# An unnormalised first column pair of w_in between two halves of the PLE rows, h in two lagged steps, and T1 of w_out split ahead of B22

## The chip, the core and the metric

The kernel runs on one core of one Trainium2 chip. Times are device microseconds (us) of one execution of the whole program, from the hardware profiler. TensorE does the matmuls (PE in the profile), VectorE is DVE, ScalarE is ACT, GpSimd is POOL, SyncE (SP) issues most of the DMAs. The kernel before was timed three times; the figure that counts is the median of such runs, beside the same for the changed kernel.

## The reference, cut to what matters

One layer of a decoder trunk on 1024 tokens of 1024 channels, in float32:

```python
h = rms_norm(x, g_pre)                               # x * g_pre * rsqrt(mean(x*x) + eps), per token
s5_x, s5_g, lru_x, lru_g, gate_s, gate_l = split(h @ w_in)
y_s = s5_ssm(s5_x, ...)                              # needs s5_x = the first 512 columns of w_in
z_s = (glu(gelu(y_s) @ w_glu) * silu(s5_g)) @ w_bs
z_l = (rg_lru(conv(lru_x)) * silu(lru_g)) @ w_bl
merged = sigmoid(gate_s) * z_s + sigmoid(gate_l) * z_l
x = x + rms_norm(merged @ w_out, g_post)
x = x + (p @ w_ple) * sigmoid(x @ w_ple_gate)
```

Two things in it matter here. The factor rsqrt(mean(x*x)) is one number per token, and a product h @ w is linear in it, so it may be applied to the product instead of to h. And p @ w_ple (called the PLE rows below) depends on nothing else, so it may be done at any time.

## The kernel before, in words

**Layout.** Channels lie on the 128 partitions, tokens on the free axis. x is eight tiles `xt(k)` of 128 x 1024. A column of a weight matrix is 128 output channels; its weights come in blocks of 128 x 128, and four blocks are a quad. A product over all 1024 channels is a sum over k = 0 to 7.

**Three matmuls for one.** Every float32 factor a is split into a high part of fp32r type (`hi`, a copy by ACT) and the rest (`lo` = a - hi, a subtraction, on DVE as a rule). `three` (L306) then issues three matmuls of 128 x 128 by 128 x 512: high by high (L308), high weight by low data (L309), low weight by high data (L310).

**Weights.** The class `Weights` loads raw blocks through SP into four buffers, makes the high part on ACT (L215, `make`) and the low part on DVE (L227, `lows`), in a ring of six quads `wq`. `QUADS` is the order of the quads over the whole kernel and so the order of all the weight work; `ahead` and, early on, `weights(upto)` make quads ahead of their use. For w_out a variant of Strassen's method is used: POOL forms sums of weight blocks (`wS`, L187), and the data side has the operands B11, B21, T2, T3, T1, B22 and T4, which are quarters of `merged` or their sums and differences. `op_split` (L1156) splits such an operand, the high part on ACT (L1150) or by a DVE copy (L1148), the low part on DVE (L1157).

**Order of the work.** There is no scheduler here: PE, DVE, ACT and POOL each execute in the order in which the program is written, and an instruction that waits holds all that stand behind it on its engine. Background generators in the list `bg` (S5, operand splits) are advanced one step by each `tick()`, which the matmul loops call after each group of matmuls.

The stages around the change are, in order:
- the eight PLE rows (L693 to L712), 12 matmuls each on a quad of w_ple, evacuated by ACT (L710) from one of three PSUM row buffers `pw2` to SBUF and stored in DRAM. Beside them ACT squares x (L683), DVE adds the squares up into `ssq` (`sdp`, L685) and steps through the parameter work of S5, `s5_params`, a generator of some 54 steps (`prep`), which is small DVE work until a sine table on ACT (L596, L597) and a chain on POOL (L604 to L661) that DVE waits for once (L632);
- the token statistics, `tok_rstd` (L375): PE sums the squares over the channels (L380), DVE and ACT make the reciprocal root, PE spreads it over the partitions into two PSUM banks `psb_pre` (L400);
- h: `h_hi` (L726) computes x * g_pre * rstd on DVE (L729, with the factor in PSUM) and its high part on ACT (L730), `h_build` (L732) the low parts, on DVE for the first 512 tokens and on POOL for the second (L739);
- u0, columns 0 and 1 of w_in (`two`, L343, 96 matmuls), with `h_build` called ahead of each k, then u2, columns 2 and 3, likewise. `u_out` (L745) copies a column of the result with a strided ACT instruction (L748) and stores it for S5;
- many further columns of w_in, S5, the LRU heads and the projections, which the change leaves alone but for the time at which S5 starts: its generator `s5_all` runs in the ticks behind u2;
- w_out: four products X with B11, two with B21, then per row pair the products Y (T2), Z (T3), W (T1) and V (B22), each 12 matmuls (`product`, L1263). The operands T1 and B22 are made by the generator `out_ops` (L1217), four steps in `bg` that are queued behind the four B11 products.

Of the kernel before, what the change touches and what calls it, by code (L numbers as in the profile page):

```python
# [9 lines left out]
F32 = mybir.dt.float32  # L10
# [7 lines left out]
P = 128  # L18
# [18 lines left out]
def weight_plan():  # L37
# [208 lines left out]
def tile_hybrid_trunk(  # L246
# [218 lines left out]
    sqs = [two_rows(i, f"sqs{i}") for i in (0, 1)]  # L465
    ple_sb = [two_rows(i, f"ple_sb{i}") for i in (4, 5, 13, 2)]
# [50 lines left out]
    W.fetch(7)  # L517
# [146 lines left out]
    seen = []  # L664

    def prep_steps(n):
        for _ in range(n):
            next(prep, None)

    def prep_exp(n):  # L670
        for _ in range(n):
            if not seen:
                seen.extend(["exp"] * (next(prep) == "exp"))

    def prep_until(mark):
        while next(prep, mark) != mark:
            pass

    prep_exp(24)

    def square(k):
        sq = sqs[k % 2][:, k // 2 % 2] if k else ssq
        S.activation(sq, xt(k), AF.Square)  # L683
        if 0 < k < ND - 1:
            V.tensor_tensor(ssq, ssq, sq, ALU.add)  # L685
            prep_exp(5)
        return sq

# [3 lines left out]
    squares = {0: (0,), 1: (1, 2), 2: (3,), 3: (4,), 4: (5, 6), 5: (7,)}  # L692
    for m in range(ND):  # L693
        if m % 2 == 0:
            wb = W.next()
        if m == 7:
            prep_exp(100)
            next(stats)
# [4 lines left out]
        for k in squares.get(m, ()):  # L703
            sq = square(k)
            if k == ND - 1:
                ssqs.append(sq)
        if m == 7:
            next(stats)
        sb = ple_sb[m // 2][:, m % 2]
        S.activation(sb, ps, AF.Copy)  # L710
        nc.sync.dma_start(ple_d[m], sb)
        if m in (1, 3, 5, 6):  # L712
            weights({1: 2, 3: 3, 5: 5, 6: 7}[m])
        if m == 3:
            W.fetch(11)
    for _ in stats:
        pass

    hq = {n: [quarter(page(i0 + j, f"h{n}{j}")) for j in range(2)]
          for n, i0 in (("B11", 0), ("B21", 4), ("B12", 10), ("B22", 12))}  # L720

    def hplain(k, h):
        hi, lo = hq[f"B{1 + k // 4}{1 + h}"]
        return hi[:, k % 4, :], lo[:, k % 4, :]

    def h_hi(k):  # L726
        for h in range(2):
            xs = xt(k, HALF[h])
            V.scalar_tensor_tensor(xs, xs, gpre[:, k:k + 1], rb[h], ALU.mult, ALU.mult)  # L729
            S.activation(hplain(k, h)[0], xs, AF.Copy)  # L730

    def h_build(k):  # L732
        if k == 0:
            h_hi(0)
        elif 0 < k < ND - 1:
            h_hi(k + 1)
# [3 lines left out]
        if k <= 0:  # L740
            h_hi(k + 1)
        if k == ND - 1:
            prep_until("den")

    def u_out(m, ps, tile):  # L745
        for h in range(2):
            up = tile(h).rearrange("p (j k) -> p j k", j=8)
            S.activation(up.rearrange("p j k -> p k j"), ps[h].rearrange("p (k j) -> p k j", j=8), AF.Copy)  # L748
# [3 lines left out]
    ups = quarter(page(9, "ups", F32))  # L752
# [691 lines left out]
```

## Time and profile before

| | us |
|---|---|
| three runs | 981.36, 982.51, 982.83 |
| median | 982.51 |
| the profiled execution, its time | 978.07 |
| the profiled execution, its span | 976.3 |
| PE busy in the span | 948.3 |
| DVE busy | 586.0 |
| ACT busy | 455.7 |
| POOL busy | 160.5 |

How to read it: the span runs from the first instruction to the last of one profiled execution; its time holds 1.8 us more around that. PE is busy for all but 28.0 us of the span, so what a change to the order of the work can move lies in a few places: the time before PE's first matmul, the waits of PE between two matmuls, and stretches in which the clock granted to TensorE is lower. In a timeline row the first number is the start and the second the duration; a row that ends with "xN" joins N instructions of one kind. Matmuls overlap, so their rate is read from start to start.

### The profile page before, as it was taken

How to read it: one execution, taken by the hardware profiler on the slowest of the kernel's cores; microseconds unless marked ns; L12 is line 12 of the kernel's file. 1: busy time of each engine (PE TensorE's matmuls, PEld its weight loads, DVE VectorE, ACT ScalarE, POOL GpSimd, SP SyncE). 2: the span in 40 equal slices, each digit the busy share in tenths (PEclk: the TensorE clock that was granted, in tenths of full speed). 3: DMA queues.
4: the chain of work that ended last, by engine and by line, in shares of the span. 5: the costliest groups of instructions: out<-in, count | busy, mean ns of one | idle time of the engine just before them, and what ended most of it. 6: DMA issues, size and time to landing. Idle time of an engine off the chain costs nothing.

```text
span 976.3 us, 11808 instructions
## 1 busy us (share of the span) xinstructions
PE 948.3 (97%) x4304; PEld 776.9 (80%) x4304; DVE 586.0 (60%) x1017; ACT 455.7 (47%) x654; POOL 160.5 (16%) x177
## 2 busy tenths in 40 slices
PE   7899999999999999999999999999999998999988
PEld 5788777888788888888888888888888876887766
DVE  7853777888761236666666668345311577786832
ACT  7542244334432146666766665233112344458461
POOL 0255421211100000000000000000001345433431
PEclk9999999999999999999999999999999999999999
DMA  9634232333242211111111115742348995399995
GB/s 349 244 80 127 93 101 85 114 115 114 72 118 99 81 49 49 49 49 49 48 49 49 49 40 153 260 151 70 108 135 233 246 194 178 106 244 228 282 267 125
DMA packets 64282, 128.19 MB, mean 131 GB/s; under 512 B 18400, under 2 KB 29024, under 8 KB 64224
## 3 DMA queue, kind: packets, MB, share of 16 engines
q1 hardware_dynamic: 55584, 109.61, 34.4%
q0 software_dynamic: 8640, 17.83, 10.4%
q8 instruction: 34, 0.56, 0.2%
q14 instruction: 24, 0.20, 0.1%
HBM read 84.81 MB, written 27.79 MB: 115 GB/s over the span
## 4 chain that ended last, share of the span: by engine, by line
PE 74%; DVE 11%; issue 6%; DMA 4%; POOL 2%; ACT 1%; SPq 0%; POOLq 0%; DVEq 0%; ACTq 0%
PE ps_L L308 4%; PE ps_L L310 4%; PE ps_L L309 4%; PE ps_rx L308 4%; PE ps_rg L308 4%; PE ps_rg L310 4%; PE ps_rx L310 4%; PE ps_rx L309 4%; PE ps_rg L309 4%; PE ps_bl L310 4%; PE ps_bl L309 4%; PE ps_bl L308 4%; PE ps_pg L310 2%; DMA wq<-wraw 2%; PE ps_pg L309 2%
## 5 line engine op out<-in xcount | busy, mean ns | idle before, releaser
L215 ACT ACTIVATE wq<-wraw 128x512 fp32r<-128x512 f32 (+1 forms) x189 | 112.3, 607 | 96.5 <-PE ps_bl L310 77.3
L219 POOL DMA_DIRECT2D wq<-wraw x52 | 47.9, 920 | 550.6 <-ACT wq L218 527.3
L308 PE MATMUL ps_L<-hB,wq 128*128 128x512 f32 x320 | 127.2, 398 | 0.0
L310 PE MATMUL ps_L<-hB,wq 128*128 128x512 f32 x320 | 124.8, 390 | 0.0
L309 PE MATMUL ps_L<-hB,wq 128*128 128x512 f32 x320 | 124.6, 389 | 0.0
L227 DVE TENSOR_TENSOR wq<-wraw,wq 128x512 fp32r<-128x512 f32 (+1 forms) x137 | 94.5, 707 | 26.5 <-ACT wq L215 26.4
L308 PEld LDWEIGHTS ps_L<-hB,wq 128*128 128x128 f32 x320 | 60.1, 188 | 13.4 <-issue 1.7
L310 PEld LDWEIGHTS ps_L<-hB,wq 128*128 128x128 f32 x320 | 60.1, 188 | 12.9
L309 PEld LDWEIGHTS ps_L<-hB,wq 128*128 128x128 f32 x320 | 60.2, 188 | 11.8
L969 DVE SCALAR_TENSOR_TENSOR c<-ps_rx,cp_t,c 128x1023 f32<-128x1023 f32 (+2 forms) x30 | 38.5, 1282 | 43.6 <-ACT c L967 42.8
L308 PE MATMUL ps_rx<-hB,wq 128*128 128x512 f32 x160 | 62.5, 391 | 0.0
L308 PE MATMUL ps_rg<-hB,wq 128*128 128x512 f32 x160 | 62.5, 391 | 0.0
L310 PE MATMUL ps_rx<-hB,wq 128*128 128x512 f32 x160 | 62.4, 390 | 0.0
L310 PE MATMUL ps_rg<-hB,wq 128*128 128x512 f32 x160 | 62.4, 390 | 0.0
L308 PE MATMUL ps_bl<-yl,wq 128*128 128x512 f32 x160 | 62.3, 389 | 0.0
L310 PE MATMUL ps_bl<-yl,wq 128*128 128x512 f32 x160 | 62.3, 389 | 0.0
L309 PE MATMUL ps_rx<-hB,wq 128*128 128x512 f32 x160 | 62.2, 389 | 0.0
L309 PE MATMUL ps_rg<-hB,wq 128*128 128x512 f32 x160 | 62.2, 389 | 0.0
L309 PE MATMUL ps_bl<-yl,wq 128*128 128x512 f32 x160 | 62.2, 389 | 0.0
L1080 DVE TENSOR_TENSOR blg<-blg,ps_bl 128x1024 f32<-128x1024 f32 x8 | 9.8, 1222 | 68.7 <-PE ps_bl L310 68.6
L925 ACT ACTIVATE sg<-ps_L 128x1024 f32<-128x1024 f32 x20 | 20.5, 1027 | 61.9 <-PE ps_L L310 45.5
L310 PE MATMUL ps_pg<-x1hl,wq 128*128 128x512 f32 x120 | 47.3, 394 | 2.0 <-DMA wq<-wraw 2.0
(345 smaller groups left out, 2183.0 us busy)
## 6 DMA issues: line engine op xcount, KB each, us to landing
wraw<-w_blocks SPq DMA_DIRECT2D x90, 512.0 KB, 4.0
wq<-wraw POOLq DMA_DIRECT2D x52, 256.0 KB, 6.3
xt<-x_t SPq DMA_DIRECT2D x8, 512.0 KB, 7.3
ple_d<-ple_sb SPq DMA_DIRECT2D x8, 512.0 KB, 8.5
sgl_d<-sg SPq DMA_DIRECT2D x8, 512.0 KB, 4.9
sgs_d<-sg SPq DMA_DIRECT2D x8, 512.0 KB, 3.9
blg<-sgl_d SPq DMA_DIRECT2D x8, 512.0 KB, 4.6
ms_d<-blg SPq DMA_DIRECT2D x8, 512.0 KB, 2.9
```

The lines of the kernel that those rows point to most:

```text
L215: nc.scalar.activation(hi, src, AF.Copy)
L219: nc.gpsimd.dma_start(lo.bitcast(F32), src, accum_op=ALU.add)
L227: self.nc.vector.tensor_tensor(lo, src, hi.bitcast(F32), ALU.subtract)
L308: T.matmul(ps, wh, xh, start=start, stop=False, skip_group_check=more)
L309: T.matmul(ps, wh, xl, start=False, stop=False, skip_group_check=more)
L310: T.matmul(ps, wl, xh, start=False, stop=stop, skip_group_check=more)
L925: S.activation(t, ps, AF.Sigmoid)
L969: V.scalar_tensor_tensor(c[:, d:], ps[:, :NT - d], w_[3 - d], c[:, d:], ALU.mult, ALU.add)
L1080: V.tensor_tensor(gs[d], gs[d], t, ALU.mult)
```

## The change

The numbers of lines in the changed kernel are one higher than before up to some L500, and others behind that.

- **Order of the quads.** Four PLE rows, then columns 0 and 1 of w_in, then the other four PLE rows, then columns 2 and 3. The loads follow: x's first tile now comes ahead of the second pair of w_ple.
- **Warm-up.** Ten matmuls of 128 x 128 on `ones` at the start of the program.
- **u0 on x * g_pre.** After the PLE rows 0 to 3 and inside u0, `raw(k)` makes the high part of x * g_pre on ACT (128 x 1024, with the factor as the instruction's scale) and the low part in one DVE instruction (`scalar_tensor_tensor`, 128 x 1024, L690). u0 multiplies these. Its result is multiplied by the token factor when it is copied out: `u_out` for u0 is now a strided DVE multiplication (L764).
- **Squares.** Those of k = 1, 3 and 5 go from ACT to POOL (`tensor_tensor` of 128 x 1024). DVE adds all eight into `ssq`, so that PE needs 8 statistics matmuls instead of 16.
- **Statistics.** They stand on PE between k = 4 and k = 5 of u0. The factor is copied from PSUM to SBUF by ACT (`spread`), over the buffer of `ssq`, half of it at k = 7 and half behind u0.
- **h in two lagged steps.** `normed_hi(k)` is one DVE instruction of 128 x 1024 with the factor in SBUF (L751) and one ACT copy; `normed_lo(k)`, called one place later, makes the low parts on DVE and POOL as before. These stand in the PLE rows 4 to 7, between a row's matmuls and its evacuation, and ahead of each k of u2.
- **S5 parameters.** 28 steps are made in the PLE rows 0 to 3 (8, 8, 6 and 6); the rest run at the head of `s5_all` behind u2, ten to a tick, followed by four empty steps.
- **w_out.** `out_ops` becomes `t1_ops`, queued ahead of the X products, with its last k held back by two ticks, and `b22_ops`, queued behind them.

The core of the diff:

```diff
-    for m in range(0, ND, 2):
-        plain(col("w_ple", m, range(2)) + col("w_ple", m + 1, range(2)))
-    for m in range(0, NS, 2):
+    for half in range(2):
+        for m in range(4 * half, 4 * half + 4, 2):
+            plain(col("w_ple", m, range(2)) + col("w_ple", m + 1, range(2)))
+        m = 2 * half
         for ks in (range(4), range(4, ND)):
             plain(col("w_in", m, ks) + col("w_in", m + 1, ks))
...
+    for _ in range(10):
+        T.matmul(warm[:, :P], ones, ones, start=True, stop=True)
...
+    def prep_all(n):
+        for i, _ in enumerate(prep):
+            if i % n == n - 1:
+                yield
...
+    def raw(k):
+        hi, lo = hpage(k, "xg")
+        S.activation(hi, xt(k), AF.Identity, scale=gpre[:, k:k + 1])
+        V.scalar_tensor_tensor(lo, xt(k), gpre[:, k:k + 1], hi.bitcast(F32), ALU.mult, ALU.subtract)
...
     def square(k):
-        sq = sqs[k % 2][:, k // 2 % 2] if k else ssq
-        S.activation(sq, xt(k), AF.Square)
-        if 0 < k < ND - 1:
-            V.tensor_tensor(ssq, ssq, sq, ALU.add)
-            prep_exp(5)
+        sq = sqs[k % 2] if k else ssq
+        if k in (1, 3, 5):
+            G.tensor_tensor(sq, xt(k), xt(k), ALU.mult)
+        else:
+            S.activation(sq, xt(k), AF.Square)
         return sq
...
+    for m in range(4):
...
+        row = ple_row(m, wb, ple_sb[m // 2][:, m % 2])
+        next(row)
+        sq_of[m] = square(m)
+        raw(m)
+        if m:
+            add_square(sq_of[m])
+        next(row)
+        weights(m + 2)
+        prep_steps((8, 8, 6, 6)[m])
...
+    def before_u0(k):
+        if k < 4:
+            sq = square(k + 4)
+            raw(k + 4)
+            add_square(sq)
+        if k == 5:
+            next(stats)
+            next(stats)
+        if k == 7:
+            spread(0)
+
+    def normed_hi(k):
+        hi, _ = hpage(k, "h")
+        V.scalar_tensor_tensor(xt(k), xt(k), gpre[:, k:k + 1], rbs, ALU.mult, ALU.mult)
+        S.activation(hi, xt(k), AF.Copy)
+
+    def normed_lo(k):
         for h in range(2):
             hi, lo = hplain(k, h)
             (G if h else V).tensor_tensor(lo, xt(k, HALF[h]), hi.bitcast(F32), ALU.subtract)
...
+            if scaled:
+                V.tensor_tensor(dst, src, rbs[:, HALF[h]].rearrange("p (k j) -> p k j", j=8), ALU.mult)
+            else:
+                S.activation(dst, src, AF.Copy)
...
+    u01 = two(ND, hplain, "u0", before_u0, pair_of("u0"))
+    spread(1)
...
+    for m in range(4, ND):
...
+        next(row)
+        normed_hi(m - 3)
+        normed_lo(m - 4)
+        next(row)
...
     def s5_all():
+        yield from prep_all(10)
+        for _ in range(4):
+            yield
...
+    bg.append(t1_ops())
     xs = [bank(f"oX{p}") for p in range(4)]
...
-    bg.append(out_ops())
+    bg.append(b22_ops())
```

Three places where the order of an engine changes. The first is PE around the token statistics: before, they stand between the PLE rows 6 and 7, ahead of all of u0 (`pst` holds the sums, `p_hi` and `p_lo` are the split p).

```order
L310 MATMUL ps_ple6_364<-p_hi_111,wq3_316 128x512
L380 MATMUL pst_pre_385<-ones_86,sdp_109 128x1
L380 MATMUL pst_pre_385<-ones_86,sqs1_114 128x1
...
L308 MATMUL ps_ple7_402<-p_hi_111,wq3_316 128x512
L309 MATMUL ps_ple7_402<-p_lo_112,wq3_316 128x512
L310 MATMUL ps_ple7_402<-p_hi_111,wq3_316 128x512
```

After, they stand inside u0 (`ps_u00` and `ps_u01` are its two columns, `xg4` and `xg5` the split x * g_pre of k = 4 and 5).

```order
L310 MATMUL ps_u01_316<-xg4_318,wq5_299 128x512
L311 MATMUL ps_u01_316<-xg4_318,wq5_299 128x512
L381 MATMUL pst_pre_420<-ones_86,sdp_109 128x1 x8
L309 MATMUL ps_u00_315<-xg5_350,wq4_268 128x512
L310 MATMUL ps_u00_315<-xg5_350,wq4_268 128x512
```

What moved: the matmuls that need the sum of all squares had 84 PLE matmuls ahead of them, and now have 48 PLE matmuls and the first 60 of u0; behind them stand 36 matmuls of u0, the other PLE rows and u2.

The second is DVE in the same stage. After, what stands between the low part of k = 3 and the statistics is this (`xgK` the low part of x * g_pre of K, `sdp` the sum of squares, `wq` the low part of a weight quad, `braw` the buffer of a square).

```order
L690 SCALAR_TENSOR_TENSOR xg4_318<-xt1_108,cp_t_95,xg4_318 128x1024
L703 TENSOR_TENSOR sdp_109<-sdp_109,braw_116 128x1024
L228 TENSOR_TENSOR wq6_324<-wraw4_322,wq6_324 128x512
L690 SCALAR_TENSOR_TENSOR xg5_350<-xt1_108,cp_t_95,xg5_350 128x1024
L703 TENSOR_TENSOR sdp_109<-sdp_109 128x1024
L690 SCALAR_TENSOR_TENSOR xg6_367<-xt1_108,cp_t_95,xg6_367 128x1024
L703 TENSOR_TENSOR sdp_109<-sdp_109,braw_116 128x1024
L690 SCALAR_TENSOR_TENSOR xg7_384<-xt1_108,cp_t_95,xg7_384 128x1024
L703 TENSOR_TENSOR sdp_109<-sdp_109 128x1024
L228 TENSOR_TENSOR wq7_328<-wraw5_326,wq7_328 128x512
L228 TENSOR_TENSOR wq8_400<-wraw6_331,wq8_400 128x512
L385 TENSOR_SCALAR rs_pre_181<-pst_pre_420 128x8
```

What moved: each addition of a square now has a low part of x * g_pre ahead of it in DVE's order, and the one reader of the statistics (the last row) comes behind all eight of each.

The third is DVE in w_out. Before, the splits of T1 and B22 stand in one piece behind B21's last one (`mT1` is T1's operand, `mB22` is B22's, `mg` is `merged`, `wS` a sum of weights; the second index of an operand, 0 or 1, is high or low).

```order
L1157 TENSOR_TENSOR mB211_5528<-mg3_5532,mB210_5527 128x512
L227 TENSOR_TENSOR wq147_5897<-wS2_147_5876,wq147_5897 128x512
...
L1148 CAST mT10_5958<-mg1_5530 128x512
L1157 TENSOR_TENSOR mT11_5959<-mg1_5530,mT10_5958 128x512 x2
...
L1148 CAST mB220_6014<-mg2_5531 128x512
L1157 TENSOR_TENSOR mB221_6015<-mg2_5531,mB220_6014 128x512 x2
L1286 TENSOR_TENSOR mix10_5864<-mix10_5864,oY0_5995 128x512
L227 TENSOR_TENSOR wq151_5996<-wS2_151_5973,wq151_5996 128x512
```

After, T1's first three splits stand ahead of B21's last one, and all of B22's ahead of the first use of a result of the Y products (`oY0`).

```order
L1179 CAST mT10_5876<-mg0_5541 128x512
L1188 TENSOR_TENSOR mT11_5877<-mg0_5541,mT10_5876 128x512 x2
...
L1188 TENSOR_TENSOR mB211_5540<-mg3_5544,mB210_5539 128x512
L228 TENSOR_TENSOR wq147_5917<-wS2_147_5895,wq147_5917 128x512
...
L1179 CAST mB220_5980<-mg2_5543 128x512
L1188 TENSOR_TENSOR mB221_5981<-mg2_5543,mB220_5980 128x512 x2
L228 TENSOR_TENSOR wq149_5963<-wS1_147_5893,wq149_5963 128x512
L228 TENSOR_TENSOR wq150_5989<-wS2_147_5895,wq150_5989 128x512
...
L1328 TENSOR_TENSOR mix10_5883<-mix10_5883,oY0_6017 128x512
```

What moved: four DVE instructions of T1 (a copy and three low parts) now stand ahead of the low part of B21's last k, and all of B22 stands ahead of `oY0`, of which half stood behind it.

More of the change, by code (lines that the diff above doesn't have):

```diff
@@ L487, in tile_hybrid_trunk @@
     G.memset(sgn[64:], -1.0)
+    warm = px.tile([P, HT], F32, tag="px", name="warm")
+    for _ in range(10):
+        T.matmul(warm[:, :P], ones, ones, start=True, stop=True)
     def load_x(ks):
@@ L691, in tile_hybrid_trunk, with ple_row @@
     stats = tok_rstd(pro.tile([P, 4 * ND], F32, name="rs_pre"), ssqs, NT, "pre", rb, sdp[:, 1])
[L692 to L698, printed above, removed]
+    def ple_row(m, wb, sb):
         ps = wide(f"ps_ple{m}")
@@ L702, in tile_hybrid_trunk, with spread @@
                 three(ps[:, HALF[h]], wb[2 * (m % 2) + k], (p_hi[:, k, HALF[h]], p_lo[:, k, HALF[h]]), k == 0, k == 1)
[L703 to L709, printed above, removed]
+        yield
         S.activation(sb, ps, AF.Copy)
         nc.sync.dma_start(ple_d[m], sb)
[L712 to L736, printed above, removed]
+        yield
+    sq_of = {}
+    for m in range(4):
+        if m % 2 == 0:
+            wb = W.next()
+        row = ple_row(m, wb, ple_sb[m // 2][:, m % 2])
[7 more added lines that the diff above has]
+        prep_steps((8, 8, 6, 6)[m])
+    rbs = ssq
+    def spread(h):
+        next(stats)
+        S.activation(rbs[:, HALF[h]], rb[h], AF.Copy)
+    def before_u0(k):
[5 more added lines that the diff above has]
+            next(stats)
+            next(stats)
+        if k == 7:
[5 more added lines that the diff above has]
+    def normed_lo(k):
         for h in range(2):
@@ L913, in s5_all @@
     def s5_all():
+        yield from prep_all(10)
+        for _ in range(4):
+            yield
         yield from s5_table(0)
@@ L1215, in x1, with t1_ops, b22_ops @@
         return x1p[k // 2][:, k % 2, HALF[h]]
-    def out_ops():
-        for name, i, q in (("T1", 16, 11), ("B22", 7, 22)):
-            op(name, i)
-            for k in range(4):
-                op_split(name, k, mg(q, k), k % 2 == 1)
-                if k % 2:
-                    flush()
-                    yield
+    def t1_ops():
+        op("T1", 16)
+        for k in range(4):
+            if k == 3:
+                yield
+                yield
+            op_split("T1", k, mg(11, k), k % 2 == 1)
+            if k:
+                flush()
+                yield
+    def b22_ops():
+        op("B22", 7)
+        for k in range(4):
+            op_split("B22", k, mg(22, k), k % 2 == 1)
+            if k % 2:
+                flush()
+                yield
     def last_op():
```

71 lines of the change are left out of this document (35 added, 36 removed).

## The prediction

> **What bounds the kernel now.** I read the page first: the busy line, then the chain that ended last.
>
> ```profile
> PE 948.3 (97%) x4304; PEld 776.9 (80%) x4304; DVE 586.0 (60%) x1017; ACT 455.7 (47%) x654; POOL 160.5 (16%) x177
> PE 74%; DVE 11%; issue 6%; DMA 4%; POOL 2%; ACT 1%; SPq 0%; POOLq 0%; DVEq 0%; ACTq 0%
> ```
>
> PE is the bound. A change of order can only win back waits of PE or time at a low clock. Then the windows of the stages that the change touches (the long fourth one gives the rate):
>
> ```profile
> 5.00:37.90 32.90, 30.87 (x144) 24.68 (x144) 26.53 (x97) 21.82 (x30) 0.00 (x0) 1.00 0.92 362
> 37.90:49.00 11.10, 7.62 (x24) 5.35 (x24) 9.84 (x15) 7.27 (x12) 5.15 (x4) 0.85 0.46 154
> 49.00:87.50 38.50, 38.50 (x172) 31.88 (x171) 16.15 (x37) 14.38 (x22) 24.43 (x47) 1.00 0.31 83
> 300.00:790.00 490.00, 490.00 (x2149) 403.07 (x2147) 252.32 (x262) 233.38 (x297) 16.17 (x19) 1.00 0.35 102
> 817.00:828.00 11.00, 7.70 (x24) 5.67 (x25) 9.39 (x14) 4.30 (x8) 4.07 (x4) 0.84 0.44 145
> ```
>
> The columns are length, then busy time of PE, PE loads, DVE, ACT and POOL, then PEclk and DMA. In steady work a matmul takes 490/2149 = 0.228 us. The start of u0 (37.9 to 49) does 24 matmuls in 11.1 us with DVE busy for 9.84: DVE bounds it, with PEclk 0.85. The V product of w_out (817 to 828) has the same look. Last, the groups, waits and single rows that price DVE's work in the first 90 us:
>
> ```profile
> L227 DVE TENSOR_TENSOR wq<-wraw,wq 128x512 fp32r<-128x512 f32 x16 | 11.6, 732 | 13.3 <-ACT wq L215 13.3
> L685 DVE TENSOR_TENSOR sdp<-sdp,sqs 128x1024 f32<-128x1024 f32 x6 | 7.3, 1221 | 0.1
> 10.55 0.18 DVE L541 COPY scratch<-scratch 128x48 f32<-128x48 f32 x1
> 16.34 1.22 DVE L685 TENSOR_TENSOR sdp<-sdp,sqs 128x1024 f32<-128x1024 f32 x1
> 17.48 0.16 DVE L560 SCALAR_TENSOR_TENSOR scratch<-scratch 128x10 f32<-128x10 f32 x1
> 10.57 1.06 ACT L683 ACTIVATE sdp<-xt 128x1024 f32<-128x1024 f32 x1 [0.54 <-DMA xt<-x_t]
> 29.76 3.46 PE pst_pre L380 x32
> 36.12 1.80 PE psb_pre L400 x16
> 87.24 0.39 PE L310 MATMUL ps_u<-hB,wq 128*128 128x512 f32 x1
> ```
>
> An addition of 128 x 1024 takes 1.14 us of DVE (16.34 to 17.48); 24 parameter steps took 10.55 to 16.34, 0.24 each. u2 ends at 87.47, one matmul after its last start at 87.24.
>
> **Part 1: up to the end of u2.** The change lets PE start u0 on x * g_pre before the statistics. That takes away h's splits from u0's start, but puts on DVE eight low parts of 128 x 1024 and seven additions, all ahead of the statistics, which PE needs in the middle of u0. So I count DVE's work up to the last addition.
>
> Start: x's first tile and the second w_ple load change places, the same bytes, so ACT has both at 10.57. A cast (about 0.6), the square and the new high part (1.06 each at most) end at about 13.2. From there, in DVE's order: 15 instructions of 1024 at 1.15 = 17.25; five low parts of weights, 0.64 each when nothing is in the way (the mean 0.73 holds blocked ones) = 3.2; 28 steps of 0.24 = 6.8. Sum 27.2, so 40.4 with POOL idle.
>
> POOL is not idle: it makes three of the squares.
>
> ```profile
> L739 POOL TENSOR_TENSOR hB<-xt,hB 128x512 fp32r<-128x512 f32 x8 | 11.1, 1390 | 47.7 <-ACT hB L730 47.7
> 41.36 1.30 POOL L739 TENSOR_TENSOR hB<-xt,hB 128x512 fp32r<-128x512 f32 x1 [0.57 <-ACT hB L730]
> 41.83 1.38 DVE L227 TENSOR_TENSOR wq<-wraw,wq 128x512 fp32r<-128x512 f32 x1 [1.22 <-ACT wq L215]
> 45.05 1.39 DVE L729 SCALAR_TENSOR_TENSOR xt<-xt,cp_t,psb_pre 128x512 f32<-128x512 f32 x2
> 45.27 1.28 POOL L739 TENSOR_TENSOR hB<-xt,hB 128x512 fp32r<-128x512 f32 x1 [2.60 <-ACT hB L730]
> 909.94 1.62 POOL L1157 TENSOR_TENSOR x1hl<-x,x1hl 128x512 fp32r<-128x512 f32 x1
> 910.12 2.00 DVE L1325 SCALAR_TENSOR_TENSOR x<-mix,cp_t,x 128x512 f32<-128x512 f32 x1
> 912.75 0.75 DVE L1325 SCALAR_TENSOR_TENSOR x<-mix,cp_t,x 128x512 f32<-128x512 f32 x1
> 811.21 4.10 POOL L187 TENSOR_TENSOR wS<-wraw 128x512 f32<-128x512 f32 x1 [4.63 <-DVE wq L227]
> ```
>
> The DVE subtraction that began at 41.83 beside a POOL instruction ended at 43.21, 0.55 after POOL's end (42.66): it stood still till then. The product of L1325, both tensors in SBUF, takes 0.75 alone and 2.00 beside POOL. The two of L729, with one tensor in PSUM, took 1.39 beside POOL, no more than elsewhere. And POOL itself had to wait for a train of DVE instructions (4.10). So two engines with both inputs in SBUF take turns here, and the new low parts and additions are all of that kind. A square of 1024 on POOL is 2 x 1.28, less a little: 2.4. DVE's order makes the addition wait for it in any case, so it costs DVE nearly its length: 1.0 for the first, which begins before 13.2, and 2.4 each for the others, +5.8. The bounds are 0 (the squares fall into waits of DVE that I have not counted) and 7.2. I take 5.8, since I can name no gap in DVE's list: the sum of squares stands at 46.2.
>
> The Trainium skill, page "SBUF — State Buffer", section "Who interferes with whom", states this as a rule: a DVE instruction with two SBUF inputs and a GpSimd instruction that reads SBUF exclude each other for a whole instruction, one with at most one SBUF input does not. The rows of L1325 and L729 agree. It speaks against this change, which also moves the token factor from PSUM to SBUF (L751); by the reading that L729 alone suggests, no contention, the sum would stay at 40.4.
>
> From there PE has the statistics, half of 3.46 = 1.75, the spread of the factor, 1.80, and 36 + 48 + 96 = 180 matmuls of 0.2287 = 41.2. That gives 90.9. PE waits about 6 us for the statistics, and a wait lowers the clock afterwards, by these rows:
>
> ```profile
> 819.88 0.39 PE L308 MATMUL oV<-mB,wq 128*128 128x512 f32 x1
> 822.43 0.50 PE L309 MATMUL oV<-mB,wq 128*128 128x512 f32 x1 [2.16 <-DVE mB L1157]
> 823.91 0.63 PE L308 MATMUL oY<-mT,wq 128*128 128x512 f32 x1
> 827.80 0.39 PE L310 MATMUL oY<-mT,wq 128*128 128x512 f32 x1
> ```
>
> One product of twelve matmuls, from 823.91 to 827.80 and one more, took 4.12 instead of 12 x 0.2287 = 2.74, so 1.4 lost after a wait of 2.55. I take 1.5: 92.4.
>
> Then the PLE rows 4 to 7. `u_out` of u0 goes to DVE with a strided operand:
>
> ```profile
> L1110 DVE TENSOR_TENSOR ysf<-et,ps_ea x4: 2270/2270/2270, 644.7 to 677.9; 128x1024 f32<-128x1024 f32 x4
> ```
>
> That is 1.14 for 512, so four of them and some 0.3 for the factor's copy put the first h step 4.9 us after u0. Each k then costs 1.15 for the h step, 0.65 for DVE's low part and 1.3 in which POOL's low part holds DVE, 3.1. On ACT the evacuation of PLE row 6 stands behind the fourth cast of h, which ends 4.9 + 1.15 + 3 x 3.1 + 1.06 = 16.4 after u0; u2's second column needs that PSUM buffer after 54 more matmuls, 12.3, and about 1 later for a like wait on row 4's buffer: 13.3. So +3.1 (0 to 4): u2 ends at 95.5, **+8.0** against 87.47. The bounds are -0.5 (no lock, see the first rival) and +9.5.
>
> The warm-up, the earlier u0 and the fewer statistics matmuls are worth nothing beside this, since PE waits for DVE anyway.
>
> **Part 2: S5's start.** The remaining parameter steps now begin after u2.
>
> ```profile
> 58.99 1.28 ACT L596 ACT_TABLE_LOAD   x1
> 65.38 0.63 POOL L606 TENSOR_TENSOR pw<-scratch,cosp 128x32 f32<-128x32 f32 x1 [4.53 <-DVE cosp L601]
> 74.73 0.35 DVE L632 RECIPROCAL scratch<-scratch 128x32 f32<-128x32 f32 x1 [5.13 <-POOL scratch L630]
> 84.15 1.30 POOL L661 TENSOR_TENSOR bb<-bb,braw 128x512 f32<-128x512 f32 x1
> 88.64 2.00 ACT L748 ACTIVATE up<-ps_u 128x512 f32<-128x512 f32 x2
> ```
>
> ACT copies u2 out until 90.64, 3.2 after u2's end U. Then it loads the sine table (1.28) and makes the sines: POOL starts at about U + 6.2. DVE waits in L632 for 9.7 more (65.38 to 75.08), till U + 15.9. Behind it stands the low part of a quad that PE reads 120 matmuls after u2, at U + 27.4: time enough. POOL's chain takes 20.1 (65.38 to 85.45), to U + 26.3; three DVE products follow, and PE reads them 143 matmuls after u2, at U + 32.7. Some 4 us are left: **+0.3** (0 to 3, if DVE and POOL hold each other up there).
>
> **Part 3: w_out.** PE lost 2.05 and 2.55 us from start to start in the first V product, for B22's splits:
>
> ```profile
> 815.85 0.40 PE L310 MATMUL oW<-mT,wq 128*128 128x512 f32 x1
> 817.90 0.49 PE L308 MATMUL oV<-mB,wq 128*128 128x512 f32 x1 [1.65 <-ACT mB L1150]
> 813.74 0.41 DVE L1148 CAST mB<-mg 128x512 fp32r<-128x512 f32 x1
> 816.70 0.63 ACT L215 ACTIVATE wq<-wS 128x512 fp32r<-128x512 f32 x1 [5.40 <-POOL wS L187]
> 817.24 0.61 ACT L1150 ACTIVATE mB<-mg 128x512 fp32r<-128x512 f32 x1
> ```
>
> ACT's cast of B22 stood behind a weight cast that waited for POOL's sum until 816.70. With B22's splits two products earlier that is gone. But T1's first splits, a copy and three low parts, 2.3 us, go in front of B21's last low part, on a DVE that works without a break up to 814.2; I see a new wait there of 1.1. And the weight sum still limits the second Y product: it starts at about 820.05 with that, instead of 823.91, 3.86 earlier, and at full clock, 1.38 shorter. **-5.2** (the 1.1 is in it; -6.4 without the new wait, -2 if the sum slips as far).
>
> **The sum.** +8.0 + 0.3 - 5.2 = +3.1 on the span of 976.3, 979.4; the execution that was profiled took 978.07 and would take 981.2. The median of the runs, 982.51, lies 4.4 above that execution, so I add to the median: **985.6**. A difference of 0.2%, 2.0 us, is about what a measurement of this kernel tells from none.
>
> **The rivals.**
> - *Faster: the squares cost DVE nothing* (0.28). POOL's three squares would fall where DVE waits for ACT, a load or its own last result. Then the sum of squares stands at 40.4, the clock stays up, and the later coupling shrinks to 1.5 to 2, since POOL delays h less: 40.4 + 1.75 + 1.8 + 41.2 + 1.8 = 87.0, -0.5 against before. With +0.3 and -5.2 that is -5.4: 977.1. For it: DVE was busy for 26.53 of 32.9 us in the first window, not for all, and the small parameter steps wait for one another. Against: the added instructions of 1024 fill more than the gap. It decides if DVE idles for 5 us or more between 13 and 40.
> - *The tail is given back* (0.15). T1's work before B21, and POOL's sum starved by DVE's train as at 811.21, leave a gain of 0 to 2 instead of 5.2: +8.0 + 0.3 - 2 = +6.3, or +8.3: 988.8 to 990.8.
> - *It does just what it sets out to do* (0.05): PE never waits after the first PLE row. Then 288 matmuls in a row, 65.9 us from about 13.8, end u2 near 79.7, -7.8; with -5.2 and +0.3 that is -12.7: 969.8.
>
> **How the numbers follow.** My forecast has 0.50; 0.02 is left for what I have not seen. Its own range, by the bounds of its terms, is 981 to 989. The range for 8 in 10 has to take in the faster rival and most of the given-back tail: 976.0 to 990.5. Faster by over 0.2% (below 980.5): 0.27 of the first rival, the third, and the low end of the forecast, together 0.34. Slower (above 984.5): 0.33 of the forecast and the second rival, 0.48. Within: 0.18.
>
> **What would show it.** In the changed profile: a wait of PE near 40 to 46 us for the statistics, additions of squares that wait for POOL, rows of L690 well over 1.2 us beside POOL; PEclk below 1 after that; u2's end at about 95 instead of 87.5; no wait of `oV` for `mB`, and the second Y product near 820 on the old clock, 3.9 earlier against the start of the X products. I am wrong if the sum of squares stands before 42, if PE's wait there is under 2 us, or if the V product still waits.

## The result, and the profile after

| | before | after |
|---|---|---|
| median of 10 runs, us | 977.58 | 985.69 |
| lowest and highest | 976.12 to 982.83 | 983.77 to 992.86 |
| span of the profiled execution | 976.3 | 983.0 |

The ratio after/before is 1.0078, with a 95% interval of 1.0052 to 1.0105: the changed kernel is slower, by 5 to 10 us. That the forecast of 985.6 hits the time is luck in the main: it stood on three runs of before with a median of 982.5, seven further runs brought that to 977.6, and a base 4.9 too high made up for a change forecast 4.5 too small. Forecast was +3.1 us, which lies below the interval; measured are +7.6, and +6.7 between the two profiled spans. So the direction and the place were forecast, the size was not. One execution, the profiled one of the experiment `e5_t1_two_later`, ran at a granted clock of 0.415 throughout and is used nowhere.

Laid side by side by the starts of PE's matmuls, the two traces differ like this (the first start of a stage, in us):

| | before | after | difference of the stretch | forecast |
|---|---|---|---|---|
| end of u2 | 87.47 | 96.70 | +9.2 | +8.0 |
| first X product of w_out | 791.44 | 803.67 | +3.0 | +0.3 |
| second Z product | 828.03 | 836.84 | -3.4 | -5.2 |
| end of the last matmul | 971.42 | 978.37 | -1.9 | 0 |

The last stretch is not touched by the change; in it PE's waits for DMAs of weights fell from 2.0 to 0.9 us, and in the other traces they are 0.3 to 2.7. The first two stretches vary as well. Two further traces have the same code as the kernel before up to the X products (experiments 1 and 11 below): u2 ends there at 89.30 and 90.66 instead of 87.47, and from there to the first X product it takes 705.6 and 706.0 instead of 704.0. Against these the first stretch grew by 7.4 and 6.0 only, and the second by about 1. So a difference of single traces in this table is good to some 3 us, and the rows of PE's waits say what made it.

The windows of the first 96 us after, which answer to those of before (length, busy time of PE, PE loads, DVE, ACT, POOL, then PEclk, DMA share, GB/s):

```profile
5.00:40.00 35.00, 28.60 (x112) 21.21 (x110) 29.09 (x64) 21.01 (x26) 6.45 (x3) 0.96 0.81 304
40.00:50.00 10.00, 5.43 (x21) 4.91 (x21) 7.09 (x14) 3.34 (x5) 0.00 (x0) 0.67 0.27 92
50.00:96.00 46.00, 43.98 (x190) 35.48 (x189) 35.92 (x68) 16.71 (x21) 15.05 (x10) 0.95 0.37 115
```

PE's waits, the longest ones (total, times, longest):

```profile
PE pwin L872 <- DVE ta L857: 4.9, 4, 3.8
PE ps_u L310 <- DVE xg L690: 4.6, 3, 3.0
PE pst_pre L381 <- DVE sdp L703: 4.6, 1, 4.6
PE oX L310 <- DVE mB L1188: 2.2, 1, 2.2
PE ps_u L309 <- ACT ple_sc L714: 1.6, 2, 0.9
```

By 40 us PE has done 48 matmuls of the PLE rows and 60 of u0 and is busy for 28.60 of 35.00 us, where before it was for 30.87 of 32.90; then comes the stretch at a clock of 0.67. All five but those in `oX` (w_out) and `pwin` (S5's first product) lie ahead of u2's end. The wait of `oV` for `mB`, 4.1 in all before, is gone.

What leads to the wait for the statistics (`pst_pre`), on DVE, POOL and PE, and the last matmul of u2:

```profile
20.53 2.28 POOL L697 TENSOR_TENSOR sdp<-xt 128x1024 f32<-128x1024 f32 x1 [6.43 <-DVE sdp L703]
20.97 3.19 DVE L423 SCALAR_TENSOR_TENSOR scratch<-scratch 128x58 f32<-128x58 f32 x6
31.19 2.27 POOL L697 TENSOR_TENSOR sdp<-xt 128x1024 f32<-128x1024 f32 x1 [8.38 <-DVE sdp L703]
31.63 1.86 DVE L560 TENSOR_TENSOR scratch<-scratch 128x10 f32<-128x10 f32 x1
43.51 1.22 DVE L703 TENSOR_TENSOR sdp<-sdp 128x1024 f32<-128x1024 f32 x1
44.78 3.57 PE L381 MATMUL pst_pre<-ones,sdp 128*128 128x1 f32 x16 [4.57 <-DVE sdp L703]
96.47 0.39 PE L311 MATMUL ps_u<-h,wq 128*128 128x512 f32 x1
```

The last addition of a square ends at 44.73 and PE goes on at 44.78: DVE is the releaser, as forecast. A multiplication of 10 elements a partition takes 1.86 us beside POOL's square, and six small steps 3.19; eight of them took 2.00 before. Beside the three squares only three places of DVE's list are stretched visibly: the low part of k = 0 (1.57 instead of 1.28), the six steps and the multiplication, by about 0.3, 1.7 and 1.7 us, together 3.7.

### The profile page after: what moved, and what is told of

It is laid out like the page before. It is cut to its first block, busy times and chain, and to the rows that moved or that the text cites. A ratio compares the mean times of both kernels' runs of the same rounds, so it can differ in the third digit from the quotient of the medians.

```text
span 983.0 us, 11826 instructions
## 1 busy us (share of the span) xinstructions
PE 953.4 (97%) x4308; PEld 781.6 (80%) x4308; DVE 616.4 (63%) x1022; ACT 456.1 (46%) x649; POOL 167.9 (17%) x180
## 3 DMA queue, kind: packets, MB, share of 16 engines
q0 software_dynamic: 8640, 17.83, 10.2%
## 4 chain that ended last, share of the span: by engine, by line
PE 78%; DVE 14%; ACT 2%; DMA 2%; issue 2%; POOL 1%; SPq 0%; DVEq 0%; ACTq 0%; POOLq 0%
PE ps_L L309 5%; PE ps_L L310 5%; PE ps_L L311 5%; PE ps_rg L309 4%; PE ps_rx L309 4%; PE ps_rx L311 4%; PE ps_rg L311 4%; PE ps_rx L310 4%; PE ps_rg L310 4%; PE ps_bl L311 4%; PE ps_bl L309 4%; PE ps_bl L310 4%; PE ps_pg L310 2%; PE ps_pg L311 2%; PE ps_pg L309 2%
## 5 line engine op out<-in xcount | busy, mean ns | idle before, releaser
L309 PE MATMUL ps_L<-h,wq 128*128 128x512 f32 x320 | 127.8, 400 | 0.0
L310 PE MATMUL ps_L<-h,wq 128*128 128x512 f32 x320 | 125.1, 391 | 0.0
L311 PE MATMUL ps_L<-h,wq 128*128 128x512 f32 x320 | 125.1, 391 | 0.0
L309 PEld LDWEIGHTS ps_L<-h,wq 128*128 128x128 f32 x320 | 60.4, 189 | 13.5 <-issue 1.7
L311 PEld LDWEIGHTS ps_L<-h,wq 128*128 128x128 f32 x320 | 60.4, 189 | 13.0
L310 PEld LDWEIGHTS ps_L<-h,wq 128*128 128x128 f32 x320 | 60.5, 189 | 11.8
L309 PE MATMUL ps_rg<-h,wq 128*128 128x512 f32 x160 | 62.6, 391 | 0.0
L309 PE MATMUL ps_rx<-h,wq 128*128 128x512 f32 x160 | 62.5, 391 | 0.0
L311 PE MATMUL ps_rx<-h,wq 128*128 128x512 f32 x160 | 62.5, 390 | 0.0
L311 PE MATMUL ps_rg<-h,wq 128*128 128x512 f32 x160 | 62.5, 390 | 0.0
L310 PE MATMUL ps_rx<-h,wq 128*128 128x512 f32 x160 | 62.3, 389 | 0.0
L310 PE MATMUL ps_rg<-h,wq 128*128 128x512 f32 x160 | 62.3, 389 | 0.0
L311 PE MATMUL ps_pg<-x1hl,wq 128*128 128x512 f32 x120 | 47.5, 396 | 0.9 <-DMA wq<-wraw 0.9
L310 PE MATMUL ps_pg<-x1hl,wq 128*128 128x512 f32 x120 | 47.4, 395 | 0.1
```

What stands on the lines that cost most here:

```text
L309: T.matmul(ps, wh, xh, start=start, stop=False, skip_group_check=more)
L310: T.matmul(ps, wh, xl, start=False, stop=False, skip_group_check=more)
L311: T.matmul(ps, wl, xh, start=False, stop=stop, skip_group_check=more)
```

## The experiments

Each kernel was timed against the kernel before in the same session. "Against the changed kernel" is the difference of two such ratios, times 977.6 us; its own uncertainty is 3 to 3.5 us, so the rows of the traces carry the verdicts where a time alone doesn't.

**1. The w_out part alone.** The kernel before, with the last two edits of the diff only:

```diff
+    bg.append(t1_ops())
     xs = [bank(f"oX{p}") for p in range(4)]
...
-    bg.append(out_ops())
+    bg.append(b22_ops())
```

> The kernel before with the w_out part of the change alone (T1's splits queued ahead of the X products, B22's behind them). By the forecast's third term 5.2 us faster than before. By the two traces laid side by side 3.4 faster: the X products 2.5 us longer because PE waits for the last low part of B21, from the first Y product to the second 6.0 shorter. If the tail is given back (the second rival), 0 to 2 faster.

Measured: ratio 0.9968 (0.9949 to 0.9986), 3.1 us faster than before. The X products take 18.4 us instead of 16.4, the first V product starts without a wait. PE's waits there:

```profile
PE oX L309 <- DVE mB L1157: 1.7, 1, 1.7
PE oX L308 <- DVE mg L1206: 1.4, 1, 1.4
```

So the w_out part is a gain, and of the size that the traces gave, not the 5.2 of the forecast. By difference the rest of the change costs 10 to 11 us.

**2. The squares on ACT.** In `square`, the POOL branch is taken out:

```diff
-        if k in (1, 3, 5):
-            G.tensor_tensor(sq, xt(k), xt(k), ALU.mult)
-        else:
-            S.activation(sq, xt(k), AF.Square)
+        S.activation(sq, xt(k), AF.Square)
```

> The changed kernel with the squares of k = 1, 3 and 5 on ACT instead of POOL. If POOL's squares hold DVE, DVE gets back the 0.3, 1.7 and 1.7 us by which its instructions beside them ran over: the last addition ends near 41.0 instead of 44.7, PE's wait for the statistics falls from 4.6 to about 1 us, the clock stays higher, and the kernel is 3.5 to 6 us faster than the changed one. If the squares cost DVE nothing (the first rival), or if ACT then becomes late with the high parts, the last addition stays at 44 or later and the time stays within 1 us.

Measured: ratio 1.0044 (1.0021 to 1.0067), 3.3 us faster than the changed kernel, which the times alone hardly tell from none; u2 ends at 91.82 instead of 96.70. DVE and PE at the statistics:

```profile
39.98 1.22 DVE L700 TENSOR_TENSOR sdp<-sdp 128x1024 f32<-128x1024 f32 x1
41.25 3.57 PE L381 MATMUL pst_pre<-ones,sdp 128*128 128x1 f32 x16 [5.92 <-DVE sdp L700]
```

The last addition ends at 41.20 instead of 44.73. This is the test of the first rival, and it falls: POOL's squares cost DVE 3.5 us. What I had wrong is the wait behind it. I expected it to shrink to 1 us; it grew to 5.92, since PE too comes earlier to this place: its waits for low parts of x * g_pre fell from 4.6 to 1.0 in all. The statistics are late for PE even without POOL.

**3. PE kept busy in front of the statistics.**

```diff
         if k == 5:
+            for _ in range(20):
+                T.matmul(warm[:, :P], ones, ones, start=True, stop=True)
             next(stats)
```

> The changed kernel with 20 more matmuls of 128 x 128 on ones on PE, in front of the statistics, where PE waits 4.6 us. They take some 4.6 us at full clock. If the low clock behind that wait costs what its rows say (the statistics 3.57 instead of 1.75, the next 14 matmuls 0.425 instead of 0.2287 each), the kernel is 4 to 4.5 us faster than the changed one, with the last addition still near 44.7. If the clock falls for another reason than PE's waiting, or if PE's time there isn't the bound, it stays the same or loses up to 1 us.

Measured: ratio 1.0029 (1.0013 to 1.0046), 4.8 us faster than the changed kernel. The window from 40 to 50 us and the rows:

```profile
40.00:50.00 10.00, 10.00 (x73) 9.25 (x72) 8.41 (x20) 3.22 (x5) 0.00 (x0) 1.00 0.25 79
```

```profile
40.04 4.63 PE L745 MATMUL warm<-ones 128*128 128x128 f32 x40
44.56 1.95 PE L381 MATMUL pst_pre<-ones,sdp 128*128 128x1 f32 x16
```

Twenty useless matmuls in a wait that they fill exactly make the kernel faster: the statistics take 1.95 instead of 3.57, the granted clock is 1.00 instead of 0.67, and u2 ends at 92.06 instead of 96.70. From the start of the statistics to u2's end it takes 47.50 us instead of 51.92, so the low clock behind this wait cost 4.4 us (the other 0.2 is that the statistics started earlier). In the traces of experiments 2, 4, 6, 7 and 8, where PE also waits here (4.4 to 5.9 us), the same stretch up to PLE row 4 is 3.1 to 4.2 longer than in this one, so 4.4 is the upper end. Nor is the wait shown to be the whole cause: in the changed kernel the clock had fallen before it began, in the matmuls behind PE's wait for the low part of k = 4.

```profile
36.05 0.50 PE L310 MATMUL ps_u<-xg,wq 128*128 128x512 f32 x1 [2.99 <-DVE xg L690]
38.73 0.63 PE L309 MATMUL ps_u<-xg,wq 128*128 128x512 f32 x1
```

From 37.45 on these matmuls follow each other at 0.43 us until PE has nothing to do. In the execution of experiment 3 the clock fell at 36.5 and was back at 39.80, before the twenty matmuls began.

**4. The parameter steps in u2.** The steps that the change had put behind u2 go into two ticks late in u2; S5's matmuls keep their places on PE:

```diff
     def s5_all():
-        yield from prep_all(10)
-        for _ in range(4):
+        for _ in range(6):
             yield
...
+    def prep_rest():
+        for _ in range(4):
+            yield
+        yield from prep_all(13)
+
+    bg.append(prep_rest())
     u2, u3 = two(ND, hplain, "u2", before_u2, pair_of("u2"))
```

> The changed kernel with the remaining S5 parameter steps made in two ticks late in u2 instead of behind it, S5's matmuls at the same places of PE's order. If S5's late start makes PE's wait of 3.8 us at its first product (pwin), the sines come some 4 us earlier, that wait falls under 0.5, and the kernel is 2.5 to 3.5 us faster than the changed one. If the wait comes from DVE's table steps alone, which stand in the same order as before, it stays, and the time is the same within 1 us.

Measured: ratio 1.0031 (1.0013 to 1.0048), 4.6 us faster than the changed kernel. From u2's end to the first X product it takes 702.6 us instead of 707.0 (before: 704.0).

```profile
PE pwin L878 <- DVE ta L863: 2.1, 4, 0.9
```

The longest wait of `pwin` falls from 3.8 to 0.9; of the 4.4 us, 2.8 are this wait and 1.3 the matmuls behind it, which follow each other at 0.43 us for five of them in the changed kernel and not here. Why its operand came so late in the changed kernel is seen on POOL and DVE there:

```profile
102.83 0.63 POOL L611 TENSOR_TENSOR pw<-scratch,cosp 128x32 f32<-128x32 f32 x1 [12.41 <-DVE cosp L606]
120.94 1.62 POOL L666 TENSOR_TENSOR bb<-bb,braw 128x512 f32<-128x512 f32 x1
```

```profile
111.77 0.35 DVE L637 RECIPROCAL scratch<-scratch 128x32 f32<-128x32 f32 x1 [8.43 <-POOL scratch L635]
124.92 1.26 DVE L826 TENSOR_TENSOR tt<-tt,sb 128x64 f32<-128x64 f32 x1
126.22 1.67 DVE L823 TENSOR_TENSOR tt<-tt,cosp 128x256 f32<-128x256 f32 x1
129.74 0.28 DVE L826 TENSOR_TENSOR tt<-tt,sb 128x128 f32<-128x128 f32 x1
130.55 1.01 DVE L855 TENSOR_TENSOR ta<-pw,bb 128x512 f32<-128x512 f32 x1
```

POOL's chain runs as forecast, 102.83 to 122.56, U + 25.9. But the products start 8 us after it, at 130.55: behind the reciprocal stand some 30 small steps of the S5 table, and beside POOL, which goes on with S5's own work from 122.53, they take up to 1.7 us each; one of 128 elements takes 0.28 when POOL is idle, one of 64 beside one of POOL's 1.26. From the first to the last of these steps it takes 16.7 us, and took 5.8 before the change (91.08 to 96.91), when POOL was idle. The edit does not shorten this train; it lets POOL's chain begin earlier against u2's end, 2.3 us behind it instead of 6.1:

```profile
98.46 0.25 POOL L611 TENSOR_TENSOR pw<-scratch,cosp 128x32 f32<-128x32 f32 x1 [8.57 <-DVE cosp L606]
```

**5 and 11. T1 two ticks later.** The w_out part alone, with T1's splits begun behind B21's:

```diff
     def t1_ops():
+        for _ in range(2):
+            yield
         op("T1", 16)
         for k in range(4):
-            if k == 3:
-                yield
-                yield
```

> The kernel before with the w_out part alone, and T1's splits begun two ticks later (and without the two empty ticks ahead of its last k), so that B21's last low part has none of T1 ahead of it on DVE. If T1's first splits make PE's wait of 1.65 us in the X products (seen with the w_out part alone), that wait falls under 0.3 and the kernel is 4.5 to 5.5 us faster than before, the forecast's third term without the new wait. If that wait has another cause (POOL's weight sum, which holds DVE there), it stays, and the kernel is 3 faster as with the w_out part alone; if T1 or B22 then come late, less than 3.

> The kernel before with the w_out part and T1 two ticks later, as run already, for a profile at full clock. If T1's first splits made the wait of 1.65 us in the X products, it is gone; since the time was 1.7 us below before and not 4.5, a new wait of about 3 us must then stand in the Y, Z, W or V products, for T1 or B22. If the wait in X is still there, its cause is POOL's weight sum.

Measured: ratio 0.9983 (0.9964 to 1.0001), 1.7 us faster than before, no better than the w_out part alone (0.9949 to 0.9986; the intervals overlap). The second look, one execution of 981.58 us, shows why; PE's rows of it:

```profile
816.75 0.50 PE L310 MATMUL oZ<-mT,wq 128*128 128x512 f32 x1 [0.29 <-DVE wq L227]
819.95 0.50 PE L310 MATMUL oW<-mT,wq 128*128 128x512 f32 x1 [0.17 <-DVE wq L227]
825.39 0.50 PE L309 MATMUL oV<-mB,wq 128*128 128x512 f32 x1 [0.58 <-DVE mB L1157]
827.19 0.50 PE L310 MATMUL oY<-mT,wq 128*128 128x512 f32 x1 [0.59 <-DVE wq L227]
```

The wait in the X products is gone, 16.4 us for them as before the change: T1's first splits were its cause. But four small waits in Z, W, V and Y take its place. From start to start these products take 3.32, 3.20, 3.61 and 3.62 instead of 2.76, 2.75, 2.77 and 3.30 with the w_out part alone, 2.2 in all for the 1.9 won. DVE is busy for 17.83 of 17.88 us there:

```profile
813.12:831.00 17.88, 16.26 (x68) 12.10 (x67) 17.83 (x24) 9.09 (x17) 7.25 (x6) 1.00 0.57 194
```

So with these two orders of DVE's work, the order only chooses where PE waits, and about 2 us of the forecast's third term stay with DVE.

**6. The parameter steps behind the statistics.**

```diff
         weights(m + 2)
-        prep_steps((8, 8, 6, 6)[m])
...
             spread(0)
+            prep_steps(28)
```

> The changed kernel with the 28 parameter steps moved out of the PLE rows 0 to 3 to a place behind the statistics on DVE (at k = 7 of u0, where DVE is idle for 9 us). If DVE's list ahead of the statistics is the bound, as the forecast has it, the last addition comes 5 to 7 us earlier (38 to 40 instead of 44.7), and the kernel is 4.5 to 7 us faster than the changed one. If the steps only filled gaps in which DVE waits for ACT or loads, the last addition moves by less than 2 us and so does the time.

Measured: ratio 1.0019 (1.0002 to 1.0036), 5.8 us faster than the changed kernel; u2 ends at 90.43, 6.3 earlier. On DVE:

```profile
26.82 2.91 DVE L690 SCALAR_TENSOR_TENSOR xg<-xt,cp_t,xg 128x1024 fp32r<-128x1024 f32 x1
37.41 1.22 DVE L703 TENSOR_TENSOR sdp<-sdp 128x1024 f32<-128x1024 f32 x1
```

The last addition ends at 38.63, 6.1 earlier: the 28 steps stood on the bound, 0.22 each net of what POOL does to them. The third of POOL's squares now meets a low part, 2.91 us instead of 1.28.

**7. No warm-up.** The ten matmuls at the start are taken out.

> The changed kernel without the ten matmuls at its start. By the forecast they are worth nothing, since PE waits for DVE some 30 us later: the same time within 1 us, the last addition at 44.7 as before. If the clock at the start mattered, PE would be later with the first rows and ACT's evacuations with it, 1 to 3 us slower.

Measured: ratio 1.0083 (1.0059 to 1.0108), the same as the changed kernel; u2 ends at 96.49 against 96.70. The edit is worth nothing, as forecast.

**8. Both low parts of h on DVE.**

```diff
-            (G if h else V).tensor_tensor(lo, xt(k, HALF[h]), hi.bitcast(F32), ALU.subtract)
+            V.tensor_tensor(lo, xt(k, HALF[h]), hi.bitcast(F32), ALU.subtract)
```

> The changed kernel with both low parts of h on DVE, none on POOL, in the PLE rows 4 to 7 and u2. If POOL's low parts hold DVE (rows of 1.79 instead of 0.69 and 2.29 instead of 1.28 there), DVE's work for a k falls from about 3.0 to 2.4 us although it has one instruction more, PE's three waits for evacuations there (2.0 in all) shrink to about 0.5, and the kernel is 1 to 2 us faster. If the two engines worked side by side, DVE has 0.6 more to do for each k, and the kernel is 1 to 4 us slower.

Measured: ratio 1.0053 (1.0035 to 1.0070), 2.4 us faster than the changed kernel by the medians, with intervals that overlap. The changed kernel's DVE, one k, and PE's wait there are shown first, then the same here:

```profile
67.71 1.79 DVE L757 TENSOR_TENSOR h<-xt,h 128x512 fp32r<-128x512 f32 x1
69.42 2.29 DVE L751 SCALAR_TENSOR_TENSOR xt<-xt,cp_t,sdp 128x1024 f32<-128x1024 f32 x1
```

```profile
66.26 1.29 DVE L757 TENSOR_TENSOR h<-xt,h 128x512 fp32r<-128x512 f32 x2
67.46 1.28 DVE L751 SCALAR_TENSOR_TENSOR xt<-xt,cp_t,sdp 128x1024 f32<-128x1024 f32 x1
PE ps_u L309 <- ACT ple_sc L714: 1.0, 1, 1.0
```

Two low parts on DVE take 1.29, less than one beside POOL (1.79). PE's waits for the evacuations fall from 2.0 to 1.4 in all. u2 ends 2.4 earlier, but the stage that the edit touches, from PLE row 4 to u2's end, gives only 0.9 of that (34.74 us instead of 35.66; it takes 35.7 in every trace with POOL's low parts and 34.7 to 34.8 in every one without); the rest lies ahead of it, where the two kernels are the same, mostly in how long the clock stayed low behind the statistics. So the low parts on DVE are worth about 0.9 us: work taken off DVE and given to POOL here costs DVE more than it saves.

**9 and 10. All of it mended.** The changed kernel with the edits of 2 and 8, the 28 steps left out of the PLE rows so that all steps stand late in u2 (as in 4), and the statistics later on PE:

```diff
-        if k == 5:
+        if k == 6:
             next(stats)
             next(stats)
-        if k == 7:
-            spread(0)
...
+    spread(0)
     spread(1)
```

and in the tenth kernel `k == 7` in the first of these lines.

> The changed kernel with every cost that the runs so far have priced taken out: the squares on ACT, both low parts of h on DVE, all parameter steps late in u2, the statistics on PE one place later (ahead of k = 6 of u0, the spread of the factor behind u0). If these costs are what hid the gain of the early u0, the last addition ends at 36 to 37, PE waits for the statistics under 1 us, the clock stays full, u2 ends at 80 to 82 instead of 96.7 (87.5 before the change), PE's wait of 3.8 at S5's first product falls under 1, and with the w_out part the kernel is 9 to 12 us faster than before. If the early u0 has a cost of its own that is still unknown (PE waits elsewhere, above all for PSUM row buffers behind u0), u2 ends at 85 or later and the kernel is 3 to 6 faster, little more than the w_out part alone.

> The same with the statistics ahead of k = 7. If the last addition still comes after PE's k = 6 there, this removes a wait and a low clock, and is 1 to 3 us faster than with k = 6; if it comes in time anyway, the factor is only later by up to 2.7 us, the copies of u0 with it, and it is 0 to 2 us slower.

Measured: with k = 6 a ratio of 0.9992 (0.9976 to 1.0009), no change against before; with k = 7 a ratio of 0.9921 (0.9899 to 0.9943), 7.7 us faster than before. The 9 to 12 us expected of k = 6 are not there, and k = 7 is ahead of it by more than the 1 to 3 expected (6.9 by the ratios, 4.8 by the spans). With k = 6, DVE and PE:

```profile
33.22 1.28 DVE L690 SCALAR_TENSOR_TENSOR xg<-xt,cp_t,xg 128x1024 fp32r<-128x1024 f32 x1 [2.91 <-ACT xg L689]
39.09 1.22 DVE L700 TENSOR_TENSOR sdp<-sdp 128x1024 f32<-128x1024 f32 x1
40.36 1.95 PE L381 MATMUL pst_pre<-ones,sdp 128*128 128x1 f32 x16 [2.99 <-DVE sdp L700]
```

I expected the last addition at 36 to 37; it ends at 40.31. With its steps gone DVE waits for ACT instead (2.91 for the high part of k = 4), and ACT now has three squares more and weight casts that wait for their loads. So squares on ACT were right for the changed kernel and probably wrong for this one: with them on POOL and the steps gone (experiment 6) the addition ended at 38.63. The mended kernel with squares on POOL was not run. With k = 7 PE's row is this:

```profile
40.18 1.95 PE L381 MATMUL pst_pre<-ones,sdp 128*128 128x1 f32 x16 [0.29 <-DVE sdp L700]
PE pwin L873 <- issue: 4.8, 1, 4.8
```

The wait is 0.29, and u2 ends at 82.91, 4.6 earlier than before the change. Between the two traces u2's end explains 2.9 of the 4.8 us by which the spans differ, and 1.9 lie in w_out, where the two kernels are the same: PE waited there 2.26 instead of 1.39 for the same low part, and the product behind that wait took 4.08 instead of 2.75. Why they differ I can't explain. The wait in S5 has stayed (the view names no releaser; DVE's product `ta` ends at 120.42 and PE goes on at 120.52). All 54 parameter steps now stand in u2, and they end so late that POOL's chain begins 6.2 behind u2's end again, as in the changed kernel and not as in experiment 4:

```profile
89.14 0.25 POOL L611 TENSOR_TENSOR pw<-scratch,cosp 128x32 f32<-128x32 f32 x1 [86.97 <-DVE cosp L606]
```

**12. S5 one tick later.** The tenth kernel with seven empty steps instead of six at the head of `s5_all`.

> The kernel with all of it mended and the statistics ahead of k = 7, and one more empty step at the head of S5, so that its first product stands 24 matmuls (5.5 us) later in PE's order. PE waited 4.8 us there, for three DVE products behind a train of 30 small table steps that POOL's instructions stretch to 17 us. If that wait is lateness alone, it is gone with the later place, and the kernel is 3.5 to 5 us faster than without it, 11 to 13 faster than before. If DVE and POOL simply fall back by as much (since the later ticks also issue their work later), the wait stays and the time is the same within 1 us.

Measured: ratio 0.9919 (0.9896 to 0.9943), by its ratio the same as without. The wait fell to 1.9:

```profile
PE pwin L873 <- issue: 1.9, 1, 1.9
```

Neither expectation holds: of the 5.5 us by which the place moved, 2.9 came off the wait. From u2's end to the first X product it took 2.6 us less, but the times don't tell the two kernels apart. The cause was not followed further.

## Why the prediction was right or wrong, step by step

- **"DVE's list up to the last addition, 27.2 us, to 40.4 with POOL idle": right.** With POOL idle it ended at 41.20 (experiment 2), and taking 28 steps off it moved it by 6.1 (6.8 forecast).
- **"POOL's squares cost DVE +5.8": right in kind, too large.** 3.5 us by experiment 2, and 3.7 by the stretched rows. A square took 1.89 to 2.28 us, not 2.4. The first square, at 12.20, fell mostly into time in which DVE waited for ACT (0.3 instead of 1.0), and the others met chains of small steps, which lost 1.7 of POOL's 2.28. Of the rows of L690 that I named as a sign only the first was stretched (1.57). The row of L1325, from which I took the kind of the contention, decided rightly against that of L729. The Trainium skill's rule on page "SBUF — State Buffer", section "Who interferes with whom", is borne out by these runs, even for a multiplication of 10 elements (1.86 us).
- **"A wait lowers the clock afterwards, 1.5": the term that was mis-sized most ahead of u2's end.** Experiment 3 gives 4.4. I took the price from 12 matmuls behind the V product. Here the 16 instructions of the statistics themselves ran slowly (3.57 instead of 1.95), and then another 13 matmuls at 0.425. The clock had also fallen before this wait began, so the price is not that of the wait alone; the last section has more on this.
- **"+3.1 for the PLE rows 4 to 7": about right.** From PLE row 4 to u2's end it took 35.66 us, 2.7 more than 144 matmuls at 0.2287; PE's three waits there, 0.40, 0.88 and 0.74, are 2.0 of it. The sum of this part, +8.0 forecast and +9.2 measured, hides errors of opposite sign: the sum of squares came 1.5 earlier than forecast (44.73, not 46.2), this stage was 0.4 cheaper, and the clock 2.9 dearer.
- **"S5's start +0.3 (0 to 3)": the step that failed.** It was +3.0 by the two traces, and PE's wait of 3.8 at `pwin`, 0.5 before and 1.3 in experiment 1, is the cause that the rows name. The sentence "three DVE products follow" left out the table steps that stand between the reciprocal and those products on DVE, and that POOL was still at work beside them, so that they took 16.7 us and not 5.8. My upper bound names the mechanism, but I gave it no weight. In experiment 4, where POOL's chain begins 3.8 earlier against u2's end, the wait falls to 0.9.
- **"w_out -5.2": right in sign, too large.** -3.4 by the traces, -3.1 alone. The new wait in the X products, 1.1 forecast, was 2.2 (1.7 alone) and cost 2.4 from start to start, and the second Y product took 3.2 instead of 2.74 for a late low part of weights; together that is the missing 1.8. (The "2.05 and 2.55 lost" are from start to start and hold a matmul of 0.23 each; the waits were 1.65 and 2.16.) The other order that experiment 11 tried got no more.
- **The rivals.** The first (squares cost nothing) falls by experiment 2, the second (the tail given back) by experiment 1, the third (no wait at all) by the trace. What spoke for the third is kept by experiment 10: with the costs taken out, u2 does end earlier than before the change (82.91 against 87.47 to 90.66), though 3 us later than the 79.7 of a row without any wait.
- **The base.** I forecast against 982.5; with 977.6 the same sum would have given 980.7, 5 us short of the measured 985.7, and the range, moved along, would have ended at 985.6, just below it.

## What to carry to other kernels

Work that lets an engine start early is paid for by the engine that prepares it: count that engine's whole in-order list up to the next point where the first one must wait for it, down to the small steps, before counting the gain. A square or a low part given to POOL is not free when DVE works on two SBUF tensors beside it; in this kernel DVE did the low parts faster alone. And a wait of PE should be priced with the clock behind it: if a wait can't be removed, move the reader back (ahead of k = 7 instead of k = 5 here; k = 6 was not far enough) or fill the wait.

## What the runs showed of the hardware that was not expected

In the changed kernel 4.4 us were lost to a lower clock behind PE's wait of 4.6 us for the statistics, which 20 matmuls that nobody reads won back. From the start of the statistics the clock stayed low for 9 us, as these rows show.

```profile
48.22 0.77 PE L309 MATMUL ps_u<-xg,wq 128*128 128x512 f32 x1
53.48 0.63 PE L309 MATMUL ps_u<-xg,wq 128*128 128x512 f32 x1
```

The loss does not follow the length of the wait. Behind the longer wait of 5.92 in experiment 2 only 6 matmuls were slow, not 13. And behind the statistics it was low in some executions without any such wait. The tenth kernel waited 0.29, its statistics ran at full rate (1.95), and seven of the matmuls behind them were slow; the twelfth has the same code up to there and waited 0.27, and none was slow. Before the change PE did not wait for the statistics at all: in the profiled execution the matmuls behind them were fast, in that of experiment 11, the same code up to there, the whole next PLE row was slow. The rows are from the tenth, the twelfth, the kernel before and experiment 11, in this order.

```profile
45.13 0.63 PE L311 MATMUL ps_u<-xg,wq 128*128 128x512 f32 x1
42.06 0.39 PE L310 MATMUL ps_u<-xg,wq 128*128 128x512 f32 x1
33.09 0.49 PE L308 MATMUL ps_ple<-p_hi,wq 128*128 128x512 f32 x1
38.41 0.63 PE L310 MATMUL ps_ple<-p_hi,wq 128*128 128x512 f32 x1
```

So a low clock behind the statistics needs no wait in front of them, and the same code has it in one execution and not in the next; this is most of the 3 us by which u2's end varies. Whether it is the shape of these instructions (128 x 1) or something else that lets the clock fall was not tried. The second surprise is how little of an instruction is needed to be held: a DVE instruction on 10 elements took 1.7 us longer beside a POOL square, as much as a low part of 128 x 1024 did in experiment 6 (2.91 instead of 1.28).
